# Turning the retention's keys before they are split, and asking for the turns of the attention's weights two key blocks at a time

## The chip, the cores and the metric

One core of a Trainium2 chip runs the whole program. The metric is the time of one execution on the device in microseconds. TensorE (PE in the profile) multiplies and turns 128x128 blocks, ScalarE (ACT) and VectorE (DVE) do the elementwise work, GpSimd (POOL) a few small steps, and SyncE's queue (SP) starts the transfers. An instruction of TensorE writes a bank: one of the 128x512 float32 accumulators, of which the kernel names eight, two for each of the tags ma, mb, z and o.

## The reference

Two layers over 1024 tokens of 1024 features, all in float32. Layer 0 is a retention with four heads (keys and queries 256 wide, values 512 wide); layer 1 a stick-breaking attention with eight heads (keys 128 wide, values 256 wide) over keys and values that are computed once after layer 0.

```python
# layer 0, for each chunk of 128 tokens of a head
scores = jnp.einsum('bhid,bhjd->bhij', qc, kc) * intra_decay
o = jnp.einsum('bhij,bhje->bhie', scores, vc)
o = o + jnp.einsum('bhid,bhde->bhie', qc * q_decay[None, :, :, None], state)
state = state * chunk_decay[None, :, None, None] + jnp.einsum('bhjd,bhje->bhde', kc * k_decay[None, :, :, None], vc)
...
# layer 1, for each block of 128 queries
z = jnp.einsum('bhqd,bhkd->bhqk', qb, k) * scale
log_not = jnp.where(causal, jax.nn.log_sigmoid(-z), 0.0)
suffix = lax.cumsum(log_not, axis=3, reverse=True) - log_not
weights = jnp.where(causal, jnp.exp(jax.nn.log_sigmoid(z) + suffix), 0.0)
return jnp.einsum('bhqk,bhke->bhqe', weights, v)
```

Around each layer stand a normalisation before and after, a gate (`silu(g)`), and an output projection that is added to the residual.

## The kernel before, in words

**Numbers in two halves.** Every float32 operand x of a multiplication is kept as a high half (x copied to float32r by ACT, line 516) and a low half (x less the high one, by DVE, line 517). This is `split`. A product is then three multiplications into one bank: high by high, high by low, low by high (`mm3`, lines 412 to 417). With few exceptions TensorE's work is such triples, 512 columns wide.

**Halves and phases.** The tokens are worked in two halves t = 0, 1 of 512. First come the projections of layer 0 (class `Values` and class `Feature`, which form seven products where a plain 2x2 split would need eight), then eight retention units `Ret(t, h)`, then the projections of layer 1, then eight attention units `Att(t, pr)`, each a pair of heads hh = 0, 1, and the end in `finish`.

**A retention unit.** `scores` (lines 619 to 686) returns a list of steps: `rope` for the keys and the queries (six DVE instructions of 128x512 each, then two splits), and for the first half of the tokens four calls of `kt` and two of `pair`. `kt(tb)` turns block tb of the keys, from features by tokens to tokens by features: four turns on TensorE, high and low half of two 128-wide parts, into one z bank (line 650, with the identity in float32r), and one ACT copy of the bank, 128x512, into a tile `vo` (line 653). The turned keys are the left operand when `carry` (line 699) sums up the state that the second half of the tokens starts from. `pair` makes the masked scores. `mix` is the sum over values and state, `gate` turns the result (line 772) and splits it. The keys of the four units with t = 0 are turned; those with t = 1 are not, as no state follows.

**An attention unit.** `rows` (line 1205) makes, for each of four query blocks, the scores into a z bank, two sigmoids, and the running product along the keys; the weights lie as queries by keys. `mix(hh)` (line 1242) goes over the key blocks: four for t = 0, eight for t = 1. `turn(i)` fetches the values of block i, turns up to four 128x128 blocks of weights into a z bank (line 1264, float32 with the float32 identity) and splits them into a tile `AT` (three buffers). `mul(i)` multiplies them with the values into two o banks: two triples. In `step`, the turn of block i is asked for ahead of the multiplication of block i - 2 (`SKEW = 2`). Own blocks s of the same half need only 4 - s turns: 16 + 10 turns for a head with t = 1, 10 for one with t = 0, 8 x 26 + 8 x 10 = 288 in all.

**The order of the work.** `merge` puts the steps of one unit beside those of its neighbours: while head n is mixed, the scores of head n + 1 and the output projection of head n - 1 are asked for in between (lines 1513 and 1579). What stands in the program is then laid out anew by a planner, `arrange`. It reads all instructions, gives each a duration from a table of its own (`_time`: a turn of either type counts 110 ns, a multiplication of 512 columns 227 ns), and places them one by one on their engines by how late each may be. Buffers of a tag are given out in the order in which the program asked for them. It does this five times and keeps the shortest plan, whose order then binds every queue, SP's too. So a change in the program's order can move instructions anywhere.

**The end.** `finish` makes the last projection in two halves of 256 tokens, th = 0, 1. `chunk(th, c)` adds the last product to group c and squares it; `acc` takes the squares of groups 0 to 6, and `box["q"]` holds the tile with the last squares. `col(th)` sums `acc` and `box["q"]` over the partitions on TensorE (lines 1359 and 1361), `row` spreads the result, `write` scales, adds the residual and stores. The steps of the first half's end run between the chunks of the second half (`merge(second, (tail(0), 1, 1))`), so `col(0)` there reads the tile that `chunk(1, 1)` has put into `box["q"]`.

Of the kernel before, what the change touches and what calls it, by code (L numbers as in the profile page):

```python
# [308 lines left out]
def trunk(ctx, tc, xT, wts, gains, trig, ident_in, cols, out):  # L309
# [13 lines left out]
    def S(tag, shape, dt=F32):  # L323
        cnt[0] += 1
        x = sb.tile([128] + list(shape), dt, tag=tag, name=f"{tag}{cnt[0]}", bufs=BUFS[tag])
        tag_of[x[:].tensor.name] = tag
        return x
# [25 lines left out]
    def hl(tag):  # L353
        return S(tag, [2, 512], F32R)
# [20 lines left out]
    ident = sb.tile([128, 128], F32, name="ident")  # L375
    identr = sb.tile([128, 128], F32R, name="identr")
    onesr = sb.tile([128, 128], F32R, name="onesr")
# [14 lines left out]
    def late_constants():  # L392
        dma(ident[:], ident_in)
        dma(cc[:], cols)
        V.tensor_copy(identr[:], ident[:])

# [213 lines left out]
    class Ret:  # L610
# [8 lines left out]
        def scores(self):  # L619
# [4 lines left out]
            def rope(which):  # L624
                if self.h == 0 and which == 1:
                    box[0], box[1] = S("tab", [512]), S("tab", [512])
                    for i in range(2):
                        dma(box[i][:], trig[i, :, HT * self.t:HT * self.t + HT])
                    tabs[:] = [box[0], box[1]]
                cos, sin = tabs  # L630
                x = S("S", [2, 512])
                for i in range(2):
                    dma(x[:, i], qa_d[self.t][self.h][2 * which + i][:])
                a, b = S("f2", [512]), S("f2", [512])
                V.tensor_tensor(a[:], x[:, 0], cos[:], ALU.mult)
                V.tensor_tensor(b[:], x[:, 1], sin[:], ALU.mult)
                V.tensor_tensor(x[:, 0], x[:, 0], sin[:], ALU.mult)
                V.tensor_tensor(x[:, 1], x[:, 1], cos[:], ALU.mult)
                V.tensor_tensor(a[:], a[:], b[:], ALU.subtract)
                V.tensor_tensor(x[:, 0], x[:, 0], x[:, 1], ALU.add)  # L640
                for i, r in enumerate((a[:], x[:, 0])):
                    y = (q, k)[which][i] = hl("xh")
                    split((y[:, 0, :], y[:, 1, :]), r)

            box = {}
            def kt(tb):
                p = PS("z")
                for l in range(2):
                    for d in range(2):
                        nc.tensor.transpose(p[:, 256 * l + 128 * d:256 * l + 128 * d + 128].bitcast(F32R),  # L650
                                            k[d][:, l, 128 * tb:128 * tb + 128], identr[:])
                n = S("vo", [2, 256], F32R)
                A_.activation(n[:].rearrange("p a b -> p (a b)"), p[:], AF.Copy)
                self.kn.append(n)

# [28 lines left out]
            if self.t == 0:  # L684
                return ropes + [lambda tb=tb: kt(tb) for tb in range(4)] + [lambda c=c: pair(c) for c in range(2)]
            return ropes + [lambda jb=jb: score(jb) for jb in range(4)]
# [504 lines left out]
    class Att:  # L1191
# [50 lines left out]
        def mix(self, hh):  # L1242
# [5 lines left out]

            def turn(i):
                own, s = blocks[i]  # L1250
                t0 = s if own else 0
                c0 = (self.off if own else 0) + 128 * s
                if not own:
                    vo = S("vo", [2, 256], F32R)
                    dma(flat(vo), v_d[0][self.pr][s][:, 512 * hh:512 * hh + 512])
                    vv[i] = (vo[:, 0, :], vo[:, 1, :])
                else:
                    if hh == 0:
                        x = self.v[s] = S("v", [2, 2, 256], F32R)
                        dma(x[:].rearrange("p h l e -> p (h l e)"), v_d[self.t][self.pr][s][:])  # L1260
                    vv[i] = (self.v[s][:, hh, 0, :], self.v[s][:, hh, 1, :])
                p = PS("z")
                for tb in range(t0, 4):
                    nc.tensor.transpose(p[:, 128 * tb:128 * tb + 128], self.A[hh][tb][:, c0:c0 + 128], ident[:])  # L1264
                at[i] = hl("AT")
                tl = slice(128 * t0, 512)
                split((at[i][:, 0, tl], at[i][:, 1, tl]), p[:, tl])

# [9 lines left out]

            def step(i):
                if i < nb:  # L1280
                    turn(i)
                if i >= SKEW:
                    mul(i - SKEW)

# [10 lines left out]

            return [lambda i=i: step(i) for i in range(nb + SKEW)] + [gate]

# [26 lines left out]
    def finish(t, P, ys):  # L1324
# [14 lines left out]
        def chunk(th, c):  # L1339
# [11 lines left out]
            if 0 < c < 7:  # L1351
                V.tensor_tensor(acc[:, tl], acc[:, tl], q, ALU.add)
            box["q"] = q

        def col(th):
# [4 lines left out]
            for b in range(2):  # L1360
                MM(p[:, b:b + 1], box["q"][:, 128 * b:128 * b + 128], mean[:, 0:1], start=False, stop=b == 1, skip_group_check=True)
            if th:
# [85 lines left out]
    def layer_a():  # L1448
# [36 lines left out]
        sc = []  # L1485
        for k in range(8):
            at[end - 4 + k // 2].append(lambda k=k: (sc or sc.extend(heads[0].scores()), sc[k]()))
# [173 lines left out]
```

## Time and profile before

| | |
|---|---|
| median of 3 runs | 1640.17 us (1639.99 to 1640.32) |
| the profiled execution | 1640.03 us, its span 1638.3 us |
| TensorE's granted clock | 0.997 |
| PE, DVE, ACT, POOL busy | 1623.9, 1221.6, 813.2, 127.0 us |
| turns of the keys (line 650) | 64, float32r |
| turns of the gated output (line 772) | 128, float32 |
| turns of the attention's weights (line 1264) | 288, float32 |

The span is the time from the first instruction to the last. A row of the timeline has start, length, engine, line, operation, what it writes and reads with its shape, and how many in a row were put together. Matmuls overlap and their ends are modelled, so the distance of two starts is the time to count. A row of the stretches has the stretch, its length, then for PE, PEld (the loading of the stationary operand), DVE, ACT and POOL the busy time and the number of instructions, then TensorE's granted clock, the share of the transfers' engines and GB/s. A row of the waits has who waited, for whom, the sum in us, how often, and the longest. A row of the groups has line, engine, operation, tiles, shape and count, then busy time, mean length in ns, idle time before them and what ended it.

### The profile page before, as it was taken

To read this page: it belongs to the slowest core of one execution; us is meant where nothing else is said; L and a number is where in the kernel's file an instruction comes from. 1 tells how busy PE (TensorE), PEld (TensorE's weight loads), DVE (VectorE), ACT (ScalarE), POOL (GpSimd) and SP (SyncE) were. 2 spreads that over 40 slices of the span, in tenths; PEclk is the share of its full clock that TensorE was granted. 3 is DMA by queue.
4 is the path that set the end of the run, shared out by engine and by line. 5 is a ranking of instruction groups with operands and counts; after the bars stand their busy time and mean duration, and the time that the engine had idled before them with its cause. 6 is when DMAs were issued, how large, how long until landed. Compare 5 with 4: busy or idle time off the path is not lost.

```text
span 1638.3 us, 22664 instructions
## 1 busy us (share of the span) xinstructions
PE 1623.9 (99%) x7735; PEld 1356.5 (83%) x7735; DVE 1221.6 (75%) x1995; ACT 813.2 (50%) x1551; POOL 127.0 (8%) x274
## 2 busy tenths in 40 slices
PE   9999999999999999999999999999999999999997
PEld 7888888888888888888878888888888888888887
DVE  7997866644678867898789877767658667778765
ACT  7653334433356544544346665566644433554434
POOL 0000000000012211221000000000001111011101
PEclk9999999999999999999999999999999999999999
DMA  8557755543287877676776788978237877869751
GB/s 305 199 156 264 248 201 198 205 154 117 95 290 250 294 254 255 230 253 210 247 269 231 255 314 294 334 286 301 103 129 274 312 274 248 291 231 313 274 210 52
DMA packets 167683, 385.92 MB, mean 236 GB/s; under 512 B 17936, under 2 KB 20112, under 8 KB 165008
## 3 DMA queue, kind: packets, MB, share of 16 engines
q1 hardware_dynamic: 167568, 384.48, 67.9%
q8 instruction: 61, 1.00, 0.2%
q14 instruction: 54, 0.44, 0.1%
HBM read 263.29 MB, written 121.11 MB: 235 GB/s over the span
## 4 chain that ended last, share of the span: by engine, by line
PE 95%; DVE 1%; DMA 1%; ACT 1%; issue 0%; SPq 0%; POOL 0%; DVEq 0%; ACTq 0%
PE pma L417 12%; PE pma L415 12%; PE pma L416 12%; PE pmb L415 9%; PE pmb L416 9%; PE pmb L417 9%; PE po L416 6%; PE po L417 6%; PE po L415 6%; PE pz L417 3%; PE pz L416 3%; PE pz L415 3%; PE pz L1264 2%; PE pz L772 1%; DMA wraw<-in_wts_dram 1%
## 5 line engine op out<-in xcount | busy, mean ns | idle before, releaser
L516 ACT ACTIVATE whl<-wraw 128x512 fp32r<-128x512 f32 x266 | 156.8, 625 | 180.1 <-issue 62.9
L517 DVE TENSOR_TENSOR whl<-wraw,whl 128x512 fp32r<-128x512 f32 x266 | 175.8, 686 | 82.8 <-ACT whl L516 80.5
L1236 DVE TENSOR_TENSOR_SCAN sgn<-sgn 128x128 f32<-128x128 f32 (+3 forms) x64 | 86.6, 1354 | 17.9 <-POOL sgn L1234 17.9
L517 DVE TENSOR_TENSOR AT<-pz,AT 128x512 fp32r<-128x512 f32 (+1 forms) x96 | 51.2, 552 | 50.7 <-ACT AT L516 50.4
L415 PE MATMUL pmb<-oT,whl 128*128 128x512 f32 x224 | 88.7, 396 | 0.0
L416 PE MATMUL pmb<-oT,whl 128*128 128x512 f32 x224 | 88.0, 393 | 0.0
L417 PE MATMUL pmb<-oT,whl 128*128 128x512 f32 x224 | 87.9, 392 | 0.0
L516 ACT ACTIVATE AT<-pz 128x512 fp32r<-128x512 f32 (+1 forms) x96 | 45.0, 491 | 72.1 <-PE pz L1264 71.1
L415 PE MATMUL pmb<-qk,whl 128*128 128x512 f32 x200 | 78.8, 394 | 0.0
L417 PE MATMUL pmb<-qk,whl 128*128 128x512 f32 x200 | 78.3, 392 | 0.0
L416 PE MATMUL pmb<-qk,whl 128*128 128x512 f32 x200 | 78.3, 391 | 0.0
L517 DVE TENSOR_TENSOR whl<-vo,whl 128x512 fp32r<-128x512 f32 x62 | 41.6, 687 | 38.1 <-ACT whl L516 37.9
L886 ACT ACTIVATE f<-pma 128x512 f32<-128x512 f32 x52 | 30.7, 595 | 51.6 <-PE pma L417 51.2
L516 ACT ACTIVATE whl<-vo 128x512 fp32r<-128x512 f32 x62 | 37.6, 625 | 34.6 <-PE pma L417 17.5
L1233 POOL TENSOR_SCALAR_AFFINE_SELECT A<-A 128x128 f32<-128x128 f32 x32 | 11.9, 371 | 535.2 <-DMA ko<-k 396.0
L415 PE MATMUL pma<-xh,whl 128*128 128x512 f32 x136 | 53.2, 391 | 0.0
L417 PE MATMUL pma<-xh,whl 128*128 128x512 f32 x136 | 53.1, 390 | 0.0
L416 PE MATMUL pma<-xh,whl 128*128 128x512 f32 x136 | 52.9, 389 | 0.0
L416 PE MATMUL pma<-qk,whl 128*128 128x512 f32 (+1 forms) x136 | 52.0, 382 | 0.0
L417 PE MATMUL pma<-qk,whl 128*128 128x512 f32 (+1 forms) x136 | 51.9, 382 | 0.0
L415 PE MATMUL pma<-qk,whl 128*128 128x512 f32 (+1 forms) x136 | 51.6, 384 | 0.0
L415 PE MATMUL pma<-oT,whl 128*128 128x512 f32 x128 | 50.6, 399 | 0.0
(581 smaller groups left out, 5068.0 us busy)
## 6 DMA issues: line engine op xcount, KB each, us to landing
wraw<-in_wts_dram SPq DMA_DIRECT2D x332, 256.0 KB, 4.0
whl<-w SPq DMA_DIRECT2D x58, 512.0 KB, 5.6
vo<-in_wts_dram SPq DMA_DIRECT2D x70, 256.0 KB, 4.2
xh<-k SPq DMA_DIRECT2D x32, 512.0 KB, 7.0
v<-v SPq DMA_DIRECT2D x32, 512.0 KB, 5.4
k<-A SPq DMA_DIRECT2D x21, 512.0 KB, 5.1
e<-whl SPq DMA_DIRECT2D x10, 1024.0 KB, 6.3
whl<-e SPq DMA_DIRECT2D x10, 1024.0 KB, 6.2
```

What stands on the lines that cost most here:

```text
L415: MM(p, lh, rh, start=start, stop=False, **kw)
L416: MM(p, lh, rl, start=False, stop=False, **kw)
L417: MM(p, ll, rh, start=False, stop=stop, **kw)
L516: A_.activation(dst[0], src, AF.Copy)
L517: V.tensor_tensor(dst[1], src, f32(dst[0]), ALU.subtract)
L772: nc.tensor.transpose(pt[:, 128 * e:128 * e + 128], on[:, 128 * e:128 * e + 128], ident[:])
L886: A_.activation(c[:], p[:], AF.Copy)
L1233: first = G.affine_select(a[:, dg], a[:, dg], [[-1, 128]], ALU.is_gt, 0.0, base=0, channel_multiplier=1)
L1236: V.tensor_tensor_scan(n[:, :W][:, ::-1], n[:, :W][:, ::-1], n[:, :W][:, ::-1], 1.0, ALU.mult, ALU.bypass)
L1264: nc.tensor.transpose(p[:, 128 * tb:128 * tb + 128], self.A[hh][tb][:, c0:c0 + 128], ident[:])
```

## The change

Three places change. The keys are turned before they are split: `rope` keeps the two unsplit float32 parts of the keys in `raws`; `kt(c)` turns the two parts of two blocks into one z bank (four turns, float32 identity) and then splits each block out of the bank into its `vo` tile: two ACT copies and two DVE subtractions of 128x256. There are two calls for each head instead of four, and the float32r identity goes with the DVE copy that made it. In the attention, `turn` is taken apart into `fetch`, `turn` and `part`; for an even i, block i - 2 is multiplied, then blocks i and i + 1 are fetched and turned, both ahead of their splits; for an odd i only block i - 2 is multiplied. In the end, the tile with the last squares is kept for each half of the tokens, so that `col(0)` reads that of its own half.

```diff
-        V.tensor_copy(identr[:], ident[:])
...
-                for i, r in enumerate((a[:], x[:, 0])):
+                raws[which] = a[:], x[:, 0]
+                for i, r in enumerate(raws[which]):
                     y = (q, k)[which][i] = hl("xh")
                     split((y[:, 0, :], y[:, 1, :]), r)
...
-            box = {}
-            def kt(tb):
+            box, raws = {}, {}
+
+            def kt(c):
                 p = PS("z")
-                for l in range(2):
+                for j in range(2):
+                    tb = 2 * c + j
                     for d in range(2):
-                        nc.tensor.transpose(p[:, 256 * l + 128 * d:256 * l + 128 * d + 128].bitcast(F32R),
-                                            k[d][:, l, 128 * tb:128 * tb + 128], identr[:])
-                n = S("vo", [2, 256], F32R)
-                A_.activation(n[:].rearrange("p a b -> p (a b)"), p[:], AF.Copy)
-                self.kn.append(n)
+                        nc.tensor.transpose(p[:, 256 * j + 128 * d:256 * j + 128 * d + 128], raws[1][d][:, 128 * tb:128 * tb + 128], ident[:])
+                for j in range(2):
+                    n = S("vo", [2, 256], F32R)
+                    split((n[:, 0, :], n[:, 1, :]), p[:, 256 * j:256 * j + 256])
+                    self.kn.append(n)
...
-                return ropes + [lambda tb=tb: kt(tb) for tb in range(4)] + [lambda c=c: pair(c) for c in range(2)]
+                return ropes + [lambda c=c: kt(c) for c in range(2)] + [lambda c=c: pair(c) for c in range(2)]
...
-            def turn(i):
+            def fetch(i):
                 own, s = blocks[i]
-                t0 = s if own else 0
-                c0 = (self.off if own else 0) + 128 * s
                 if not own:
                     vo = S("vo", [2, 256], F32R)
...
-                p = PS("z")
+
+            def turn(i):
+                own, s = blocks[i]
+                t0 = s if own else 0
+                c0 = (self.off if own else 0) + 128 * s
+                p = box["p", i] = PS("z")
                 for tb in range(t0, 4):
                     nc.tensor.transpose(p[:, 128 * tb:128 * tb + 128], self.A[hh][tb][:, c0:c0 + 128], ident[:])
+
+            def part(i):
+                own, s = blocks[i]
                 at[i] = hl("AT")
-                tl = slice(128 * t0, 512)
-                split((at[i][:, 0, tl], at[i][:, 1, tl]), p[:, tl])
+                tl = slice(128 * (s if own else 0), 512)
+                split((at[i][:, 0, tl], at[i][:, 1, tl]), box["p", i][:, tl])
...
-            def step(i):
-                if i < nb:
-                    turn(i)
-                if i >= SKEW:
-                    mul(i - SKEW)
+            def even(i):
+                if i:
+                    mul(i - 2)
+                if i < nb:
+                    for k in (i, i + 1):
+                        fetch(k)
+                        turn(k)
+                    for k in (i, i + 1):
+                        part(k)
+
+            def odd(i):
+                if i > 1:
+                    mul(i - 2)
...
-            return [lambda i=i: step(i) for i in range(nb + SKEW)] + [gate]
+            return [lambda i=i: (odd if i % 2 else even)(i) for i in range(nb + 2) if i != 1] + [gate]
...
-            box["q"] = q
+            box["q", th] = q
...
-                MM(p[:, b:b + 1], box["q"][:, 128 * b:128 * b + 128], mean[:, 0:1], start=False, stop=b == 1, skip_group_check=True)
+                MM(p[:, b:b + 1], box["q", th][:, 128 * b:128 * b + 128], mean[:, 0:1], start=False, stop=b == 1, skip_group_check=True)
...
-        for k in range(8):
+        for k in range(6):
             at[end - 4 + k // 2].append(lambda k=k: (sc or sc.extend(heads[0].scores()), sc[k]()))
```

More of the change, by code (lines that the diff above doesn't have):

```diff
@@ L375, in trunk @@
     ident = sb.tile([128, 128], F32, name="ident")
-    identr = sb.tile([128, 128], F32R, name="identr")
     onesr = sb.tile([128, 128], F32R, name="onesr")
```

## The prediction

> **What bounds the kernel now.** I read the page first, then the busy times by stretches, then the waits of TensorE, then single stretches of its timeline.
>
> ```profile
> span 1638.3 us, 22664 instructions
> PE 1623.9 (99%) x7735; PEld 1356.5 (83%) x7735; DVE 1221.6 (75%) x1995; ACT 813.2 (50%) x1551; POOL 127.0 (8%) x274
> PE 95%; DVE 1%; DMA 1%; ACT 1%; issue 0%; SPq 0%; POOL 0%; DVEq 0%; ACTq 0%
> ```
>
> TensorE is busy for 99% of the span, and 95% of the chain that ended last runs over it. So what an edit gives is what it takes off TensorE's own row of work, less the waits that it opens there. The stretches say where a wait could still be removed.
>
> ```profile
> 440.00:590.00 150.00, 149.50 (x769) 125.81 (x768) 120.76 (x218) 84.44 (x157) 29.75 (x58) 1.00 0.76 260
> 1235.00:1420.00 185.00, 184.84 (x963) 156.96 (x962) 129.66 (x199) 78.67 (x176) 25.07 (x74) 1.00 0.80 283
> 1420.00:1600.00 180.00, 180.00 (x951) 152.62 (x950) 138.28 (x175) 82.35 (x174) 17.31 (x49) 1.00 0.74 255
> 1600.00:1639.00 39.00, 28.53 (x230) 27.71 (x228) 22.05 (x46) 16.91 (x36) 8.08 (x7) 0.91 0.16 55
> ```
>
> The columns after the length are busy time of PE, PEld, DVE, ACT and POOL, then the granted clock. The retention's keys are turned in the first row's stretch: PE idles 0.5 us of 150 there. The attention's weights are turned in the second and third: 0.16 us idle of 365. The last row is the end, where PE idles some 10 us behind the last sums. The waits of TensorE say the same one by one:
>
> ```profile
> PE po L415 <- ACT sgn L752: 0.9, 1, 0.9
> PE pz L415 <- DVE sc L517: 0.5, 1, 0.5
> PE po L415 <- DVE f L890: 0.3, 1, 0.3
> ```
>
> Between the opening and the end these three, 1.7 us, are all that the list names. None is in the attention. A gain must therefore come from fewer or cheaper TensorE instructions.
>
> **Part 1, the keys.** Before, four heads each turn the high and the low half of four blocks: 4 x 4 x 4 = 64 turns of float32r, in groups of four. After, the unsplit keys are turned: 4 heads x 2 calls x 4 = 32 turns of float32, in eight groups of four. The form that goes is in the first fence below, the form that comes is today's turn of the attention's weights, in the second (same 128x128 shape, float32 in, float32 identity).
>
> ```profile
> L650 PE MATMUL pz<-identr,xh x64: 220/246/306, 448.3 to 567.0; 128*128 128x128 f32 x64
> 478.65 0.39 PE L416 MATMUL pma<-xh,whl 128*128 128x512 f32 x1
> ...
> 480.92 0.40 PE L417 MATMUL pma<-xh,whl 128*128 128x512 f32 x1
> 481.15 0.46 PE L650 MATMUL pz<-identr,xh 128*128 128x128 f32 x4
> 481.44 0.47 PE L415 MATMUL pmb<-xh,whl 128*128 128x512 f32 x1
> 481.75 0.39 PE L416 MATMUL pmb<-xh,whl 128*128 128x512 f32 x1
> ```
>
> ```profile
> 1295.14 0.39 PE L415 MATMUL pma<-oT,whl 128*128 128x512 f32 x1
> 1295.37 0.60 PE L1264 MATMUL pz<-ident,xh 128*128 128x128 f32 x4
> 1295.72 0.47 PE L416 MATMUL pma<-oT,whl 128*128 128x512 f32 x1
> 1296.04 0.39 PE L417 MATMUL pma<-oT,whl 128*128 128x512 f32 x1
> ```
>
> Starts count here, as ends are modelled and overlap. From 478.65 to 480.92 ten multiplications of 512 columns start, so one takes 0.227 us. From the last one before a group to the second one behind it lie two of these and the group: float32r 481.75 - 480.92 - 0.454 = 0.376 us for four (0.094 each), float32 1296.04 - 1295.14 - 0.454 = 0.446 us for four (0.1115 each). So 16 x 0.376 = 6.0 us go and 8 x 0.446 = 3.6 us come: **-2.4 us**, all of it on the path, as PE has no slack around it.
>
> The Trainium skill (TensorE: Matmul & The Clock Gate, LDWEIGHTS) prices the loading of a stationary operand at its columns over 1.2, 107 ns for 128, whatever the type. The float32 turn agrees (111.5 ns); the float32r turn, 94 ns, does not, and the measurement decides. By the rule half of 64 equal turns would go, an estimate of 32 x 107 ns = 3.4 us instead of 2.4.
>
> What the turned keys cost behind PE:
>
> ```profile
> L653 ACT ACTIVATE vo<-pz 128x512 fp32r<-128x512 f32 x16 | 9.4, 594 | 8.0 <-PE pz L650 8.0
> L1349 ACT ACTIVATE f<-sc 128x256 f32<-128x256 f32 x8 | 3.3, 418 | 3.1 <-DVE sc L1347 2.9
> L1347 DVE TENSOR_TENSOR sc<-pma,sc 128x256 f32<-128x256 f32 x4 | 1.7, 419 | 0.2
> 480.00:520.00 40.00, 39.50 (x206) 33.17 (x205) 35.36 (x65) 23.66 (x44) 10.36 (x19) 1.00 0.71 244
> 520.00:560.00 40.00, 40.00 (x208) 33.63 (x207) 34.62 (x64) 24.57 (x46) 7.31 (x15) 1.00 0.82 281
> 690.00:735.00 45.00, 44.06 (x215) 36.32 (x214) 39.66 (x75) 23.32 (x43) 11.17 (x20) 1.00 0.79 269
> ```
>
> Sixteen copies of 128x512 on ACT (16 x 0.594 = 9.5 us) become 32 of 128x256 (32 x 0.418 = 13.4 us): 3.9 us more, and ACT works 24 us of 40 there, so nothing of that shows. DVE gets 32 subtractions that it did not have, about 0.42 us each by the row of the same shape out of a bank: 13.4 us, 3.4 us a head. The heads follow each other by about 40 us (three steps from 448 to 567), and DVE is already busy 35.4 and 34.6 us of 40 while heads 1 to 3 are turned (head 0 is turned earlier, in a lighter stretch). With them it comes to 38 or 39 of 40. What is queued behind the subtractions on DVE is the splitting of the weights, the ropes and the sums of the heads; PE's multiplications wait for these. The nearest row is 690 to 735: DVE at 39.66 of 45, 88%, and PE lost 0.9 us there. Bounds: nothing lost, if the splitting of weights moves into the lighter neighbours; about 1 us a head for three heads, 3 us, if it cannot. No gain is possible from more work on DVE. I take **+0.7 us**, near the row of 88%, since the overload is short. If that cover is gone altogether it is the 3 us.
>
> Small ones with one answer: the cast of the identity and its tile go (one DVE copy in the opening, 0). The unsplit keys of a head stay in their two buffers until the turns, some us longer; the next head asks for these buffers some 40 us later (0). Banks: sixteen with one copy each become eight with four readers each, 16 x (0.376 + 0.594) = 15.5 us of bank time against 8 x (0.446 + 2 x 0.418 + 2 x 0.419) = 17.0 us (0).
>
> **Part 2, the weights of the attention by pairs.** The 288 turns stay, float32 as before; so do their splits, loads and multiplications. Only the order in which they are asked for changes: two blocks, up to eight turns, one behind the other, where the groups were of one to four. The question is what a group costs beside its turns.
>
> ```profile
> 1274.61 0.39 PE L417 MATMUL pma<-oT,whl 128*128 128x512 f32 x1
> 1274.85 0.27 PE L1264 MATMUL pz<-ident,A 128*128 128x128 f32 x1
> 1274.87 0.48 PE L415 MATMUL pmb<-oT,whl 128*128 128x512 f32 x1
> 1275.19 0.40 PE L416 MATMUL pmb<-oT,whl 128*128 128x512 f32 x1
> ```
>
> A turn alone takes 1275.19 - 1274.61 - 0.454 = 0.126 us, one in a group of four 0.1115. A change between turning and multiplying costs 0.015 us at most. There are 16 half-pairs of heads, 8 with four blocks and 8 with eight, 96 groups that become 48: between 0 and 48 x 0.015 = 0.7 us, and I take **-0.3 us**, as most groups are not single. No wait goes, because none is there. What the pair could lose is under the rivals.
>
> **Part 3, the end.** The column of the first half now takes its own last squares instead of those of the second half's second group, so it may start earlier. The chain of the end begins behind the last multiplication:
>
> ```profile
> 1626.51 0.33 DVE acc L1352
> 1626.84 0.35 DVE sc L1347
> 1627.21 0.42 ACT f L1349
> 1627.68 0.62 PE pz L1361 x4
> ```
>
> Only DVE's queue of 0.33 us ahead of the last sum could shrink; the rest is one result after the other. Between 0 and -0.3 us: I take 0.
>
> **The sum.** The program's planner lays out the whole order anew, with one price, 110 ns, for a turn of either type, so single waits will sit elsewhere; with 1.7 us of them today I put that at 0 on balance and +-1 into the range. The profiled execution took 1640.03 us, 1638.3 of it span; the median of the runs, 1640.17, is 0.1 above it. 1640.03 - 2.4 - 0.3 + 0.7 = 1638.0 us, and at the median **1638.2 us**, 0.12% less. A measurement of this kernel can tell about 0.2%, 3.3 us, from no change, so this counts as the same.
>
> **Rivals.**
>
> Nothing is given back. DVE takes the subtractions in its gaps, and the new order also loses today's waits. Then -2.4 - 0.3, and up to 1.7 more: 1635.8 to 1637.5 us, and past the 0.2% line (1636.9) once 0.6 us of waits go too, or if a float32r turn truly costs what a float32 one does (16 x 0.446 = 7.1 us gone, not 6.0). For it: the attention has no wait at all, so the planner hides such things well. Against it: DVE at 88% to 96% where the work is added.
>
> DVE becomes the bound while heads 1 to 3 are turned: +3 us instead of +0.7, about 1640.5 us, no change. It decides from where the weights' splits fall behind their multiplications.
>
> Slower: the pair holds both buffers of the bank that the turns share with the next scores.
>
> ```profile
> L516 ACT ACTIVATE AT<-pz 128x512 fp32r<-128x512 f32 x48 | 27.8, 597 | 59.0 <-PE pz L1264 58.9
> L517 DVE TENSOR_TENSOR AT<-pz,AT 128x512 fp32r<-128x512 f32 x48 | 32.3, 686 | 24.6 <-ACT AT L516 24.4
> 1235.00:1600.00 365.00, 109.16 (x577) 84.73 (x577) 51.32 (x97) 123.42 (x283) 1.00 0.77 269
> ```
>
> The first bank is free 0.45 + 0.60 + 0.69 = 1.7 us after the pair's start, while PE is through with its turns after 0.9: for 0.8 us it needs work from other banks. Multiplying with the weights (twelve at most 0.227 us between two pairs, 2.7 us) and the output's sums cover that three times over. If they ran out in the 16 pairs of the first half's heads, where there are fewest, that is 16 x 0.8 = 13 us, 1651 us; from seven of the 48 pairs on (5.6 us, with the forecast's -2.0 past +3.3) it is slower by over 0.2%. The Trainium skill (Perfetto Trace Analysis, Optimization Strategy) reads the same gap repeating on the engine that should be saturated as too few buffers. The trace of before has no such gap. Against it stands the last row above, the work on these banks alone: 109 + 51 + 123 = 284 us of the two banks' 730, so they are taken 39% of the time.
>
> **How the numbers follow.** Forecast 0.62, own range 1636.9 to 1639.9 us. Nothing given back 0.24. DVE bound 0.06. Banks 0.08. The range goes from the lower end of the second, 1635.8, to 0.7 above DVE's case, 1641.2, and leaves out the banks and the outermost parts. Faster by over 0.2%: 0.24 and 0.01 of the forecast's edge; slower: the banks.
>
> **What would show it.** In the profile after: 32 float32 turns of the keys, a group of four in 0.44 to 0.46 us; PE busy down by 2 to 3 us; DVE at 37 to 39 us of 40 in the heads' stretches, with a wait or two of PE on DVE's splits; no wait of PE on the turns' bank in the attention; the last 11 us unchanged. Wrong would be a turn of the keys dearer than 0.12 us, a repeated PE wait on L516 or L517 of the weights' tile, or a PE that saves 2.7 us and loses it in the opening.

## The result and the profile after

The changed kernel takes 1641.97 us (median of 22 runs, 1639.90 to 1644.38), the kernel before 1639.69 us (22 runs, 1637.72 to 1641.15): ratio 1.0015, 95% interval [1.0009, 1.0021]. It is slower by 2.3 us; 1638.2 us was forecast, 2.0 less than the runs of before that were known then. Two more comparisons gave 1.0007 [0.9998, 1.0016] and 1.0010 [0.9999, 1.0020].

The page of the changed kernel, to be read against the first fence of the prediction:

```profile
span 1638.7 us, 22614 instructions
PE 1622.0 (99%) x7703; PEld 1353.3 (83%) x7703; DVE 1225.8 (75%) x2010; ACT 808.4 (49%) x1551; POOL 130.5 (8%) x274
PE 95%; DVE 2%; ACT 1%; DMA 1%; issue 0%; SPq 0%; POOL 0%; DVEq 0%; ACTq 0%
```

TensorE does have less to do: 32 instructions and 1.9 us of busy time fewer (1.2 to 1.9 us in three profiled executions of the changed kernel). The span is still 0.4 us longer. This profiled execution took 1640.36 us, 1.6 below its kernel's median, and that of before 1640.03, 0.3 above; so the pair shows the smaller part of the difference. The stretches show where it is. First before, then after:

```profile
440.00:600.00 160.00, 159.50 (x813) 134.09 (x812) 127.43 (x232) 87.93 (x163) 31.59 (x64) 1.00 0.77 263
600.00:1235.00 635.00, 633.67 (x2875) 524.76 (x2874) 492.40 (x833) 345.93 (x653) 41.99 (x74) 1.00 0.72 248
```

```profile
440.00:600.00 160.00, 157.64 (x775) 131.06 (x774) 131.38 (x249) 84.63 (x164) 30.82 (x63) 1.00 0.77 262
600.00:1235.00 635.00, 634.19 (x2875) 525.08 (x2874) 493.09 (x832) 346.63 (x653) 42.71 (x75) 1.00 0.71 248
1235.00:1600.00 365.00, 364.44 (x1907) 309.48 (x1906) 267.35 (x371) 158.89 (x349) 46.12 (x123) 1.00 0.77 270
```

While the retention's heads run (440 to 600), PE idles 160 - 157.64 = 2.36 us instead of 0.50. The stretch behind is no worse, and the attention, 0.56 us idle of 365, stays as good as full. DVE is busy 4 us more than before in the heads, 131.38 of 160: nowhere near full. In the two stretches for which the prediction named 37 to 39 us of 40 (480 to 520 and 520 to 560) it is busy for 34.1 and 35.2. PE's waits in the whole program, from the same trace:

```profile
...
PE pz L1374 <- DVE acc L1367: 0.9, 1, 0.9
PE pz L773 <- DVE sgn L769: 0.9, 1, 0.9
PE po L413 <- DMA v<-va: 0.6, 1, 0.6
...
PE pma L413 <- ACT qk L514: 0.5, 1, 0.5
PE pma L413 <- ACT oT L517: 0.4, 2, 0.2
PE pz L773 <- DVE vo L515: 0.4, 2, 0.2
```

The last row is new in kind: the turns of the gated output wait for a z bank until DVE has read the keys' low halves out of it. The splits of the keys, as the view of their tile `vo` has them from 440 to 600 us, after. The lower rows say what ended the idle time of an engine ahead of these instructions, with the sum in us and how often:

```profile
L514 ACT ACTIVATE vo<-pz x16: 367/385/386, 448.8 to 566.1; 128x256 fp32r<-128x256 f32 x16
L515 DVE TENSOR_TENSOR vo<-pz,vo x16: 417/425/425, 449.2 to 566.5; 128x256 fp32r<-128x256 f32 x16
...
  ACT vo L514: 6.5, 13
  DVE vo L515: 5.9, 8
  PE pz L651: 5.3, 4
```

and before, where ACT alone read the banks:

```profile
  PE pz L650: 8.0, 7
```

The rows name the releaser: DVE stood still 6.5 us for ACT's copies, and ACT 5.9 us for DVE's subtractions, once for each of the eight banks. The timeline of two banks of the changed kernel shows how (rows of other work in between are left out):

```profile
482.32 0.27 PE L651 MATMUL pz<-ident,f 128*128 128x128 f32 x1
482.43 0.27 PE L651 MATMUL pz<-ident,S 128*128 128x128 f32 x1
482.53 0.27 PE L651 MATMUL pz<-ident,f 128*128 128x128 f32 x1
482.64 0.27 PE L651 MATMUL pz<-ident,S 128*128 128x128 f32 x1
482.95 0.39 ACT L514 ACTIVATE vo<-pz 128x256 fp32r<-128x256 f32 x1
483.37 0.42 DVE L515 TENSOR_TENSOR vo<-pz,vo 128x256 fp32r<-128x256 f32 x1 [0.74 <-ACT vo L514]
483.83 0.39 ACT L514 ACTIVATE vo<-pz 128x256 fp32r<-128x256 f32 x1 [0.49 <-DVE vo L515]
484.25 0.42 DVE L515 TENSOR_TENSOR vo<-pz,vo 128x256 fp32r<-128x256 f32 x1 [0.45 <-ACT vo L514]
484.68 0.66 DVE L769 TENSOR_TENSOR sgn<-sgn,sg 128x512 f32<-128x512 f32 x1
...
487.12 0.42 DVE L515 TENSOR_TENSOR vo<-pz,vo 128x256 fp32r<-128x256 f32 x1
487.57 0.39 ACT L514 ACTIVATE vo<-pz 128x256 fp32r<-128x256 f32 x1 [1.04 <-DVE vo L515]
487.98 0.42 DVE L515 TENSOR_TENSOR vo<-pz,vo 128x256 fp32r<-128x256 f32 x1 [0.45 <-ACT vo L514]
488.56 0.63 PE L773 MATMUL pz<-ident,sgn 128*128 128x128 f32 x4 [0.15 <-DVE vo L515]
```

Two things are to be seen. The four turns start some 0.11 us apart, as forecast. And the four readers of a bank run strictly one behind the other: copy, subtraction, copy, subtraction. ACT's second copy reads other columns than DVE's first subtraction, but waits for it: the program orders any two engines on one bank, readers too. (The Trainium skill, PSUM — Partial Sum Buffer, section "PSUM bank collisions raise a hardware error", says that two engines must not be in one bank and quadrant at once, two readers no more than others, so that software has to order them. The trace agrees that they are ordered, 5.9 us of it on ACT; no run here shows what the chip does without that order.) The first bank is held from 482.32 to 484.67, 2.35 us; four of the eight are held that long and none shorter, the longest is held 4.38 us. Reckoned in the same way the eight take 22.9 us, 2.86 on average. And as the plan's order binds DVE's queue, what stands behind the subtractions there, such as the gated product at 484.68, cannot start while DVE stands still.

The cost of a turn can be read as the prediction read it, at the second of these banks:

```profile
485.26 0.40 PE L413 MATMUL pmb<-xh,whl 128*128 128x512 f32 x1
485.50 0.27 PE L651 MATMUL pz<-ident,f 128*128 128x128 f32 x1
...
485.86 0.48 PE L414 MATMUL pmb<-xh,whl 128*128 128x512 f32 x1
486.17 0.40 PE L415 MATMUL pmb<-xh,whl 128*128 128x512 f32 x1
```

Four turns take 486.17 - 485.26 - 0.454 = 0.456 us, where 0.446 was forecast.

### The profile page after: what moved, and what is told of

The parts are those of the page before. It is cut to its first block, busy times and chain, and to the rows that moved or that the text cites. A ratio compares the mean times of both kernels' runs of the same rounds, so it can differ in the third digit from the quotient of the medians.

```text
span 1638.7 us, 22614 instructions
## 1 busy us (share of the span) xinstructions
PE 1622.0 (99%) x7703; PEld 1353.3 (83%) x7703; DVE 1225.8 (75%) x2010; ACT 808.4 (49%) x1551; POOL 130.5 (8%) x274
## 4 chain that ended last, share of the span: by engine, by line
PE 95%; DVE 2%; ACT 1%; DMA 1%; issue 0%; SPq 0%; POOL 0%; DVEq 0%; ACTq 0%
PE pma L413 12%; PE pma L415 12%; PE pma L414 12%; PE pmb L413 9%; PE pmb L415 9%; PE pmb L414 9%; PE po L413 6%; PE po L415 6%; PE po L414 6%; PE pz L415 3%; PE pz L414 3%; PE pz L413 3%; PE pz L1268 2%; PE pz L773 1%; DMA A<-in_xT_dram 0%
```

## The experiments

Ratios are to the kernel before, run on the same chip in the same group, with 95% intervals; 0.001 is 1.6 us. The expectations speak of 3.1 to 4.3 us of idle time on TensorE in the changed kernel, and the busy column above gives 2.36. The column hides a part, because matmuls overlap and their ends are modelled. An estimate from the distances of the starts between 440 and 570 us, adding up what each takes above its usual distance (0.227 us for 512 columns, in proportion for fewer, 0.11 for a turn) where that is over 0.15 us, gives 0.7 us for the kernel before and 3.7, 4.3 and 3.0 us for three executions of the changed one; this is called lost by starts below.

### Parts of the change, and the change again

`e1_keys` has the keys' part alone, `e2_pairs` the pairs, `e3_end` the end, `e7_keys_end` the first and the last. Their edits are these parts of the diff:

```diff
+            def kt(c):  # e1_keys, e7_keys_end
...
+            def fetch(i):  # e2_pairs
...
+            box["q", th] = q  # e3_end, e7_keys_end
```

> The keys' part alone; the attention's order and the end as before. Theory A (the added DVE subtractions make PE wait while the heads are turned): PE busy 2 to 2.5 us less, 3 to 4 us of new PE idle between 440 and 570 us, so about all of the change's loss: +1 to +3 us against before. Rival B (the loss belongs to the pairs in the attention): 2 us faster than before, no new idle between 440 and 570. Rival C (the new order by itself, above all the values that land late before the first head): +1 to +3 us too, but with the wait on the values' transfer and not on DVE.

> The attention's pairs alone; keys and end as before. Theory A: no change, -0.5 to +0.5 us, and no PE wait on the turns' bank between 1235 and 1600 us. Rival B (the pairs hold both banks): +2 us or more, with PE idle between 1235 and 1600 us of 2 us and more. Rival C: between -1 and +1 us, with waits wherever the order moved.

> The end's part alone: the first half's column takes its own half's last squares. Theory A and rival B: no change, -0.3 to +0.3 us. Rival C (any new order costs some us): up to +-1.5 us, since the whole order is laid out anew for it.

> The changed kernel without the pairs: keys and end. If the end costs the 1.3 us that the whole change lies above the keys alone (its order makes the last column wait 0.9 instead of 0.3 us for the sum of the squares), this is at +2 us against before. If the pairs cost it, this is at +0.7 us as the keys alone.

> The changed kernel once more, beside the others of this group. Expected by every theory: +1.5 to +3.4 us against before, as measured first. If it comes nearer to the keys alone (+0.7 us), the difference between them is noise; if it stays at +2 us, the end or the pairs add some 1.3 us to the keys.

Measured: keys 1.0004 [0.9995, 1.0013], pairs 0.9998 [0.9989, 1.0007], end 1.0002 [0.9994, 1.0011], keys and end 1.0006 [0.9997, 1.0015], the whole change 1.0007 [0.9998, 1.0016]. The repetition missed its expectation on the low side: +1.2 us, nearer to the keys alone than to the first measurement. Pairs and end by themselves are not to be told from nothing. The keys' part shows the profile of the whole change (ACT idle 5.9 us and DVE 6.6 us on the banks; PE idle 2.38 us of the heads' 160) and does not save the 2.4 us that it was to save. That is 0.7 us more than before, less than the 1 to 3 us expected, but 2.4 less lay on TensorE: some 3 us are given back, and 3.8 us are lost by starts where before lost 0.7. The keys and the end together, +1.0 us, lie between the two figures that were to tell the end from the pairs, so that run does not decide. The end alone has the longer wait of the last column, which was 0.3 us before:

```profile
PE pz L1359 <- DVE acc L1352: 0.9, 1, 0.9
```

### Is it DVE's time?

The prediction's own reason was DVE's load. `e4_load` gives the kernel before DVE work on each bank, `g1_load16` half of it, `h3_sbuf` the dose of `e4_load` but read from the copied keys instead of the bank:

```diff
+                for j in range(2):  # e4_load
+                    V.tensor_tensor(n[:, j, :], p[:, 256 * j:256 * j + 256], f32(n[:, j, :]), ALU.max)
...
+                V.tensor_tensor(n[:, 1, :], p[:, 256:512], f32(n[:, 1, :]), ALU.max)  # g1_load16
...
+                for j in range(2):  # h3_sbuf
+                    V.tensor_tensor(n[:, j, :], f32(n[:, j, :]), f32(n[:, j, :]), ALU.max)
```

A slip has to be told here. The change adds 16 subtractions (four heads, four blocks), as the x16 above shows (x2010 against x1995 on the page, where the identity's copy went); the prediction counted 32, and so do the expectations of `e4_load`, `e5b_nolow` and `f1_pool`. `e4_load` is thus twice the change's dose, and `g1_load16` is the right one.

> Before, with the DVE work of the change added and the turns left as they are: behind each copy of turned keys two DVE instructions of 128x256 out of the bank write the larger of the bank and the copy, which is the copy again (32 in all). Theory A: PE busy unchanged, 2 to 4 us of new idle between 440 and 570 us, +2 to +4 us against before. Rival B: no change. Rival C: 0 to +1.5 us, unless the order moves the values' transfer.

> Before, with exactly as many DVE instructions as the change adds: 16 of 128x256 out of the bank, one behind each copy of turned keys, writing the larger of bank and copy, which is the copy again (the earlier run added 32, twice the change's number). DVE alone as the cause: PE busy unchanged, 1.5 to 3.5 us of new idle between 470 and 570 us, +1.5 to +3.5 us. If the loss needs the change's own order: less than +1 us.

> Before, with 32 more DVE instructions of 128x256 behind the copies of turned keys, as in the run that added +4 us, but these read and write the copied keys in SBUF and not the bank. If DVE's time is the cause: +3 to +4 us again, 4 us of new idle between 480 and 570 us. If the holding of the bank is: 0 to +1 us.

Measured: `e4_load` 1.0024 [1.0014, 1.0035], `g1_load16` 1.0011 [1.0002, 1.0020], `h3_sbuf` 0.9993 [0.9984, 1.0002]. The heads' stretch of `e4_load` and then of `h3_sbuf`:

```profile
440.00:600.00 160.00, 156.51 (x796) 131.20 (x795) 133.98 (x258) 86.23 (x161) 27.92 (x61) 1.00 0.74 257
```

```profile
440.00:600.00 160.00, 159.44 (x813) 134.08 (x812) 134.87 (x263) 86.80 (x161) 33.82 (x63) 1.00 0.76 261
```

`h3_sbuf` has the busier DVE, 134.87 us, and PE idles 0.56 us; `e4_load` has 133.98 and PE idles 3.49. The two differ by 5 us, with 32 instructions of 0.41 to 0.42 us in each; what differs is where they read. (The planner laid out each kernel anew, so the order of the rest differs as well.) So DVE's time is not the cause; reading the bank is. In `g1_load16`, +1.8 us as expected of DVE's time, the instructions read the bank too. In `e4_load` PE waits for the bank itself, and DVE again stands still for ACT:

```profile
PE pz L415 <- DVE vo L655: 1.2, 1, 1.2
```

```profile
  ACT vo L653: 3.3, 6
```

At the banks of `e4_load` and `g1_load16` ACT does not wait for DVE; the view of the tile names no such wait. So a loss needs no turn-taking; it is enough that DVE reads the bank behind ACT.

### Taking DVE off the bank

Three of these start from the changed kernel, `h2_keys_copy` from its keys' part alone. `e5b_nolow` leaves the low halves of the turned keys out of the computation (a second copy of the high half stands there). `f1_pool` lets GpSimd subtract, from an unsplit copy. `g2_copy` and `h2_keys_copy` copy the bank once, unsplit, by ACT, and split from the copy:

```diff
-                    split((n[:, 0, :], n[:, 1, :]), p[:, 256 * j:256 * j + 256])
+                    A_.activation(n[:], p[:, 256 * j:256 * j + 256].unsqueeze(1).broadcast_to([128, 2, 256]), AF.Copy)   # e5b_nolow
...
+                w = S("f2", [512])  # f1_pool, g2_copy, h2_keys_copy
+                A_.activation(w[:], p[:], AF.Copy)
...
+                    G.tensor_tensor(n[:, 1, :], w[:, 256 * j:256 * j + 256], f32(n[:, 0, :]), ALU.subtract)  # f1_pool
...
+                    split((n[:, 0, :], n[:, 1, :]), w[:, 256 * j:256 * j + 256])  # g2_copy, h2_keys_copy
```

> The changed kernel without the 32 DVE subtractions: one ACT copy of 128x512 writes both halves of a turned block from the bank, so the low half of the turned keys is left out and a second copy of the high half stands there. Theory A: the new idle of 3.5 us between 440 and 570 us falls to about 0.7, and the time to -1.5 to -2.5 us against before, since the 2.5 us that PE saves are now kept. Rival C (the order, the values that land late): idle and time stay as in the changed kernel, +1 to +3 us.

> The changed kernel with the low half of the turned keys made on GpSimd, which is busy 20% of the time there: ACT copies the bank unsplit to SBUF as well (128x512), and GpSimd subtracts the high half from that copy (32 of 128x256, some 0.7 us each). Theory A: DVE is as free as before, the new idle between 440 and 570 us falls from 3.5 to 1 us or less, -1 to -2 us against before. Rival C: no better than the changed kernel, +1 to +3 us. GpSimd's longer step could itself be waited for by the state's sums: then 1 to 2 us of idle on the tile of turned keys.

> The changed kernel, with the bank of turned keys copied unsplit to SBUF by ACT first (128x512), and split from there: the same 16 DVE subtractions, but the bank is free after one ACT copy. If PE waited because the bank was held until DVE came to it: the idle between 470 and 570 us falls from 3.1 us to 1 us or less, -1 to -2 us against before. If it waited because the subtractions stand in DVE's queue ahead of what PE needs: idle and time as in the changed kernel, +1 to +2 us.

> The keys' part alone, split from an unsplit copy in SBUF. If the bank is the cause and pairs and end do nothing to it: as the changed kernel with the copy, -2 to -3 us against before, with PE's 2.5 us kept. If the pairs are needed for that: 0 to -1 us.

Measured: `e5b_nolow` 0.9990 [0.9981, 0.9999], `f1_pool` 1.0010 [1.0001, 1.0019], `g2_copy` 0.9985 [0.9976, 0.9994], `h2_keys_copy` 0.9976 [0.9967, 0.9986]. `e5b_nolow` came out as expected, but it takes away DVE's work and DVE's reading of the bank together, and so does not tell them apart. `g2_copy` does more than the changed kernel, eight ACT copies of 128x512 more and the same DVE work, and is faster than both kernels. Its heads' stretch:

```profile
440.00:600.00 160.00, 159.22 (x791) 133.79 (x790) 133.78 (x252) 90.23 (x175) 29.72 (x64) 1.00 0.76 265
```

DVE and ACT are both busier than in the changed kernel (133.78 against 131.38, 90.23 against 84.63), and PE idles 0.78 us instead of 2.36. The view of the tile `vo` names no idle time ahead of the splits any more. Both copies gave more than was expected; `h2_keys_copy` saves 3.9 us, more than the 2.4 us that the turns can give, and the rest is not accounted for. `f1_pool` missed: it frees DVE, but ACT still reads the bank three times, GpSimd needs 0.72 to 1.24 us for a subtraction, and its queue becomes a wait of its own, so that it says nothing on DVE:

```profile
L657 POOL TENSOR_TENSOR vo<-f,vo x16: 720/852/1242, 448.9 to 565.6; 128x256 fp32r<-128x256 f32 x16
```

```profile
PE po L413 <- POOL sc L683: 1.4, 1, 1.4
```

### The new order

The planner's new order puts the first head's values later (the wait on `v<-va`, 0.6 us). `g3b_late` asks for the first head's scores later, so that this wait goes, and `g4_both` joins it with `g2_copy`. `h1_single` gives each block of keys a bank of its own, so that a bank has one copy and one subtraction:

```diff
-            at[end - 4 + k // 2].append(lambda k=k: (sc or sc.extend(heads[0].scores()), sc[k]()))
+            at[end - 4 + (0, 0, 1, 1, 3, 3)[k]].append(lambda k=k: (sc or sc.extend(heads[0].scores()), sc[k]()))  # g3b_late, g4_both
...
-                p = PS("z")
                 for j in range(2):
                     tb = 2 * c + j
+                    p = PS("z")  # h1_single
...
-                        nc.tensor.transpose(p[:, 256 * j + 128 * d:256 * j + 128 * d + 128], raws[1][d][:, 128 * tb:128 * tb + 128], ident[:])
+                        nc.tensor.transpose(p[:, 128 * d:128 * d + 128], raws[1][d][:, 128 * tb:128 * tb + 128], ident[:])
```

> The changed kernel, with the first head's scores asked for one step of the projections later (as far from the end as before the change), so that the last products that read the values' buffers come ahead of them again. If the values' late landing belongs to the order: the wait on their transfer near 460 us (0.6 to 1.2 us in the two profiles of the changed kernel) goes to 0 to 0.2 us, and the rest stays: 0.6 to 1.2 us less than the changed kernel, +0.3 to +1 us against before. If it comes with the keys' shorter turns whatever the order: no difference.

> The changed kernel with both: the bank copied unsplit first, and the first head's scores asked for one step later. If both causes are real, this keeps PE's 2.5 us: -1.5 to -2.5 us against before, no wait on the values' transfer, and 1 us of idle or less between 440 and 570 us. If the DVE queue is the cause whatever the bank does: +0.3 to +1 us.

> The changed kernel with one bank for each turned block instead of one for two: two turns, one ACT copy and one DVE subtraction of 128x256 for each of 16 banks. The same work on every engine, about the same sum of the banks' time, but each is held for some 1.4 us instead of 2.9. If the length of one holding makes PE wait: idle between 440 and 570 us falls from 4.3 to 1.5 us or less, -1 to -2 us against before. If the sum of the bank's time or DVE's load does: as the changed kernel, +1 to +2 us.

Measured: `g3b_late` 1.0006 [0.9997, 1.0015], `g4_both` 0.9986 [0.9977, 0.9995], `h1_single` 1.0005 [0.9996, 1.0014]. In `g3b_late` the wait on the values is gone, and one row is left in the heads:

```profile
PE pz L773 <- DVE sgn L769: 1.5, 1, 1.5
```

It has taken the place of the other (0.9 before that edit), and the time is that of the changed kernel; with `g2_copy` it adds nothing either. So the late values are not the cause. `h1_single` missed: ACT no longer waits for DVE and DVE stands 2.8 us for ACT instead of 6.5, and yet the time is that of the changed kernel. The values' wait is 1.5 us there and that on `sgn` 1.4, more than before that edit, so the run does not refute the turn-taking; but it shows that taking those waits away is not always worth time.

### Only the turn-taking

Still open was whether the loss comes from the two engines taking turns or from DVE reading the bank at all. `i1_order` (the changed kernel) and `i2_keys_order` (its keys' part) ask for both copies of a bank first, then for both subtractions:

```diff
-                    n = S("vo", [2, 256], F32R)
-                    split((n[:, 0, :], n[:, 1, :]), p[:, 256 * j:256 * j + 256])
-                    self.kn.append(n)
+                    A_.activation(ns[j][:, 0, :], p[:, 256 * j:256 * j + 256], AF.Copy)
+                for j in range(2):
+                    V.tensor_tensor(ns[j][:, 1, :], p[:, 256 * j:256 * j + 256], f32(ns[j][:, 0, :]), ALU.subtract)
+                self.kn += ns
```

The traces have the same sequence of instructions on PE, DVE, ACT and POOL as the kernels that they come from; only who waits for whom at the bank differs.

> The changed kernel, with the same instructions in the same order on every engine; only the four readers of a bank are asked for in another order: both ACT copies, then both DVE subtractions, so ACT's second copy no longer waits for DVE's first subtraction. Theory (ACT and DVE hand the bank to and fro): ACT's idle time ahead of its second copies (5.9 us over 8 banks) goes to about 0, DVE's falls from 6.5 us to some 3, a bank is held 2.3 us or less instead of 2.86, TensorE's new idle time from 440 to 560 us falls from 4.3 to 1.5 to 2 us, and the time is 1 to 2 us below that of the changed kernel, at or under the kernel before (ratio 0.9985 to 1.0005). Rival (only that DVE reads the bank at all, and it is held until then): the idle time stays at 3 to 4 us and the ratio at 1.0005 to 1.0015.

> The same edit with the keys' part of the change alone. Theory (ACT and DVE hand the bank to and fro): 1 to 2 us below the keys' part as it was, ratio to before 0.9985 to 0.9998. Rival (DVE's reading of the bank alone): as the keys' part was, 1.0000 to 1.0010.

> The changed kernel once more, beside the two others on the same chip: ratio 1.0005 to 1.0020, and the turn-taking again (ACT idle about 5.9 us, DVE idle about 6.5 us ahead of the eight banks' readers).

Measured: `i1_order` 1639.23 us, 0.9993 [0.9984, 1.0002], beside `a3_again` with 1641.34 us, 1.0010 [0.9999, 1.0020], on the same chip: 2.1 us less. `i2_keys_order` 0.9988 [0.9980, 0.9997], against 1.0004 [0.9995, 1.0013] of `e1_keys`, measured on another chip: 2.6 us less. In each pair the two intervals still overlap, by 0.0002 or 0.0003; what counts is that both pairs go the same way by about the same amount. The idle time ahead of the splits in `i1_order`, and its bank that answers to the first one shown above:

```profile
  PE pz L651: 6.7, 4
  ACT vo L654: 4.3, 5
```

```profile
481.92 0.27 PE L651 MATMUL pz<-ident,f 128*128 128x128 f32 x1
...
482.56 0.66 ACT L654 ACTIVATE vo<-pz 128x256 fp32r<-128x256 f32 x2
...
483.25 0.76 DVE L656 TENSOR_TENSOR vo<-pz,vo 128x256 fp32r<-128x256 f32 x2 [0.57 <-ACT vo L654]
484.01 0.66 DVE L771 TENSOR_TENSOR sgn<-sgn,sg 128x512 f32<-128x512 f32 x1
```

ACT's wait for DVE is gone (5.9 us), DVE's idle time falls from 6.5 to 4.3 us, the bank is held 2.09 us instead of 2.35; over the eight it is 2.36 us on average instead of 2.86, where 2.3 or less was expected. The heads' stretch of `e1_keys` and then of `i2_keys_order`:

```profile
440.00:600.00 160.00, 157.62 (x776) 131.04 (x775) 131.38 (x248) 85.33 (x165) 31.09 (x64) 1.00 0.79 265
440.00:600.00 160.00, 158.83 (x787) 133.49 (x787) 132.17 (x251) 84.67 (x165) 31.01 (x64) 1.00 0.77 265
```

PE idles 1.17 us instead of 2.38, and 1.5 us instead of 3.8 are lost by starts, which is the size of the gain in time. One row of PE waits is left in the heads of `i2_keys_order`; the waits for the bank's release are gone in both reordered kernels:

```profile
PE pz L775 <- DVE sgn L771: 1.1, 1, 1.1
```

With every engine's sequence unchanged, the turn-taking is thus shown as a cause: 2.6 of the roughly 3 us that the keys' part gave back, and 2.1 of the roughly 4 us of the whole change (`a3_again`: +1.6, where -2.4 was due). It is not all that DVE's reading costs: with the bank read once, in other groups of runs, the same two kernels are faster by another 0.0008 (`g2_copy`) and 0.0012 (`h2_keys_copy`), 1.3 and 2 us. Other figures of the expectation were missed too. DVE still stands 4.3 us, where some 3 were expected, and the profile of `i1_order`, an execution 1.7 us above its median, idles 2.11 us in the heads, about as much as `a3_again` with 1.95: the saving of that kernel is seen in its times, not in that profile.

## Why the prediction was wrong

**The keys' turns, -2.4 us: right.** By the prediction's own reckoning a group of four costs 0.45 us (0.456 at the one shown), as forecast, so 2.4 us of work are gone from TensorE. Its busy time fell by 1.2 to 1.9 us only; `h2_keys_copy`, with the same 7703 instructions, has 1619.8 us, so that the busy column must hold a part of what is lost.

**The banks, at nothing: the step that failed.** "16 x (0.376 + 0.594) = 15.5 us of bank time against 8 x (0.446 + 2 x 0.418 + 2 x 0.419) = 17.0 us (0)" compares two sums of lengths. It treated four readers as if nobody had to wait for them: reckoned from the first turn's start to the last reader's end, the banks were held 20.5 us before and 22.9 after. The prediction had a row of such waiting in front of it: at the 48 whole splits of the weights DVE stood 24.4 us for ACT, which cost nothing there, where TensorE idled 0.16 us of 365; that it would cost nothing with the keys either was taken over without a reason. In the trace each reader's engine waits at the head of its queue until the other engine has had its turn, which may itself be behind other work (the 1.04 us at 487.57), and what stands behind on DVE is late. The price of the turn-taking is 2.1 us (`i1_order` against `a3_again`) to 2.6 us (`i2_keys_order` against `e1_keys`). DVE's reading costs something without it as well, 1.3 to 2 us against the kernels that read the bank once, and 1.8 and 3.9 us where it was added to the kernel before (`g1_load16`, `e4_load`). How the loss divides between DVE standing still and the banks being held longer is not shown. The time held goes along with it: 20.5, 29.0 and 35.4 us in the kernel before, `g1_load16` and `e4_load`; 22.9, 18.9 and 11.3 us in the changed kernel, `i1_order` and `g2_copy`. But `h1_single`, with 32.0 us, loses no more than the changed kernel.

**DVE's load, +0.7 us: wrong in count and in reason.** Sixteen instructions, not 32 (the prediction's own term for the banks, 8 x 2 x 0.419, has the sixteen), and no price for DVE's time: with 32 of them on SBUF the kernel is not slower (`h3_sbuf`). The row of 690 to 735 us, from which the price was taken, had a busy DVE and an idle PE side by side; that the one made the other was an assumption. With the right count the same method would have forecast still less time, so the slip is not what turned the sign.

**ACT's copies, at nothing: wrong in count, and the cover was the wrong thing to look at.** Sixteen of 0.385 us, less than the sixteen of 0.594 before; ACT had the time, and lost 5.9 us waiting for DVE.

**The pairs, -0.3 us: cannot be seen.** 0.9998 [0.9989, 1.0007]. The order of TensorE has 86 groups of these turns, where it had 103, not 48 for 96: the planner takes the pairs apart again. At 0.015 us a change that is 17 x 0.015 = 0.3 us at most. No wait to speak of arises there (PE idles 0.56 us of 365, 0.16 before), and the rival in which the pair holds both banks fell: the only wait of PE on the weights' splits is 0.3 us, once.

**The end, 0: a little low.** Between 0 and -0.3 us was put down. The wait of the last column is 0.9 us in the profile of every kernel with the edit and 0.3 or 0.4 in every one without, so it costs some 0.5 us there; in time the end alone is 1.0002 [0.9994, 1.0011], which cannot show that.

**The rivals.** None named the way in which it went. "DVE becomes the bound" came nearest in time, 1640.5 us, and is refuted as a mechanism by `h3_sbuf`. "Nothing is given back" is about what `g2_copy` and `h2_keys_copy` show once the bank is read once: 0.9985 and 0.9976.

**What stays open.** The whole change is 1.0007 to 1.0015 where the keys alone are 1.0004; `i1_order` and `g2_copy` are 0.0005 and 0.0009 above their counterparts with the keys alone. That the other two parts cost 1 us once the keys' part is there is likely by that, and the end's longer wait would be half of it; but each step is inside the intervals, and by themselves the two parts cannot be told from nothing. The one row of waits that stays after the reordering, on `sgn`, is not explained. Nor is it settled why `g1_load16` loses 1.8 us, as its profile idles only 0.35 us more in the heads than that of before.

## What to carry to other kernels

When two engines read one accumulator bank and TensorE has no slack, try not to split it piece by piece: have one engine do all its reads first, or copy the bank once and split from the copy. Here the copy came out better although it is more work, by 1.3 and 2 us in two pairs. Where an edit gives a bank more readers, follow each reader to the head of its engine's queue and ask what stands behind it; sums of busy time do not show it, nor does bank time added up from lengths without the waits. And where a price is read from a stretch in which two things happen together, test which of them makes the other.

## What the runs showed of the hardware

- The hand-over between the engines is itself cheap in the changed kernel: ACT's copy ends at 483.34 and DVE starts at 483.37, DVE ends at 483.79 and ACT starts at 483.83, 0.03 to 0.04 us. The idle time of each is the other's 0.39 to 0.42 us, or what that one has queued ahead.
- Two copies of 128x256 in a row on ACT take 0.66 us together, two subtractions on DVE 0.76 (`i1_order`); taking turns, 2 x 0.39 and 2 x 0.42, apart from the waiting.
- Single executions of one kernel differ by more than the change is worth: 1639.90 to 1644.38 us in 22 runs of the changed kernel. One profile of each does not show the sign of 2 us; the medians of many runs do.
